# Delta-rule layer on Trainium2: low-rank products, v's transposes and bonus moved to fixed units inside later segments, eight units moved from the score fills to the end of the inverse

## The chip, the cores and the metric

The kernel runs on one core of one Trainium2 chip. The metric is device time of one execution in microseconds (us), the median of 3 runs. One profiled execution, with every instruction recorded, gives the views below.

In the views, PE is the matrix engine (TensorE), PEld its weight loads, DVE the vector engine, ACT the scalar engine, POOL GpSimd, SP the engine that issues transfers. A name such as L753 is line 753 of the kernel before; the changed kernel has line numbers of its own, some 3 to 8 higher.

## The reference, cut to what matters

One layer mixes a causal pooling branch and an RWKV-7 branch (8 heads of 64 channels, 4096 tokens). Only the second bears on the change:

```
seg = h @ w_in[...]                      # r, w_lo, k, v, a_lo, z, each shifted by mu
w_raw = w0 + tanh(w_lo) @ w_up           # low-rank product 1
decay = exp(-exp(-softplus(-w_raw) - 0.5))
a = sigmoid(a0 + a_lo @ a_up)            # low-rank product 2
kk = k*k_k / max(|k*k_k|, L2_EPS)        # per head
S_t = S_{t-1} (diag(decay_t) - kk_t^T (a_t kk_t)) + v_t^T k_t ;  y_t = S_t r_t
y = groupnorm(y)*ln_w + ln_b + sum(r*k*r_k) * v          # the last term is the bonus
out = mix(y * silu(z), pooling branch) @ w_out
```

## The kernel before, in words

A first phase (up to about 394 us of the trace) normalises, projects and pools. Then 16 **blocks** of 256 tokens follow, each of 4 **steps** (chunks of 64 tokens), with 4 head pairs. For block b three pieces run one after the other, written as Python code that the scheduler puts into one fixed queue per engine:

- `scores(b)`: for each of the 4 steps the score products `scp_sc`/`scp_px` (L660), their masking on DVE (L667), copies of the diagonal parts into `stg` on ACT (L675, tile UV). In between stand the finish of the block before (`ytp` transposes L887, the four scaled copies `mx` on ACT L889, two DVE products L890 and L891).
- `inverse(b)`: DVE inverts 32 triangular blocks of 32x32 by a chain of 30 row steps, each a multiply `Wt` (L724) and an add `W` (L729), begun by the transpose `Ab` (L706) and ended by the transposes into `MQ` (L742 to L743). PE then makes `qp` from MQ (L753), ACT copies it, PE makes `m21p` (L761). Ahead of the recurrence come the first products `px` of `lead` (L787).
- `chain(b)`: the recurrence over the 4 steps. A step is: `px` from the state S (L812), copies `xa` on ACT (L819), `psn` (L824), copies into `UV` on ACT (L832), `psn` again (L840), new S on DVE (L846), `px` from UV (L851), copies `y` on ACT (L858). After the steps 1 and 3 the group norm `gn` follows: square `ysq` on ACT (L868), sums `var` on DVE (L870, L871), a power on POOL (L873), the product `y` on DVE (L875).

These three leave PE time. It is filled with `front(b+1)`, the projection of the next block, a generator of **units**; `fill(n)` draws n units. A segment (`seg`, one 128-channel slice kS, rS, vS or zS for each head pair, and one `lo` for the low-rank inputs) is 8 units, and each unit is three fp16 matmuls of 128x257 (L552 to L554) into a tile `pj`; ACT and DVE then take the finished segment out of `pj` (L556, L557). Counts before: 20 units in scores, 88 in the inverse (12 of them by `fill(FT)` behind the row steps, 4 by `fill(FQ)` behind qp), 28 in the chain. The last block has no next front and fills with units of the output projection instead, `run(gp, ceil(n * PF))`.

Besides the segments a head pair needs in its front: the low-rank products `pl` and `pa` (L583, L584), followed by tanh `tw`, `ta`, an addition of one to `tw` (L586 to L589, ACT), a running sum `L` (L591, DVE) and two exponentials `Ppad`, `Pi` (L593, L595, ACT); the products `AR`, `BK` on DVE (L603 to L609); `cent`, which transposes and centres v by two products `vps` (L624) and copies them into UV (L630); `late`, which makes the bonus `pb` (L637) and multiplies it (`bon`, L638). The tiles pj, pl, pa, vps and pb share three buffers `ps_pj`, so a later one waits until ACT or DVE has emptied the earlier ones.

Who goes first when several engines could: PRI raises the inverse's row steps and the chain's copies, and the chain's products are held in the order in which they are written (`ordered`).

Of the kernel before, what the change touches and what calls it, by code (L numbers as in the profile page):

```python
# [10 lines left out]
F32 = mybir.dt.float32  # L11
# [3 lines left out]
AF = mybir.ActivationFunctionType  # L15
ALU = mybir.AluOpType
# [36 lines left out]
def kernel(  # L53
# [23 lines left out]

    FS, FE, FT, FQ, FA, FB, FY = 2, 2, 12, 4, 3, 2, 2
    FI = [4] * 16
# [400 lines left out]
    with ExitStack() as ph:  # L480
# [56 lines left out]
        def front(b, f):  # L537
# [3 lines left out]
            for q in range(2):  # L541
                for hx, tag, src in ((hh, "hh", hT_hi), (hl, "hl", hT_lo)):
                    ht = hp.tile([P, 4, TB2 + 1], F16, tag=tag, name=f"{tag}{b}_{q}")
                    SP.dma_start(ht, src[4 * q : 4 * q + 4, :, a0_:a1_].rearrange("k p t -> p k t"))
                    hx += [ht[:, k, :] for k in range(4)]

            def seg(m, name, bufs=2):
                pp = ps_pj.tile([P, TB2 + 1], F32, tag="pj", name=f"pj{b}_{m}")
                for k in range(KT):
                    if k:  # L550
                        yield
                    unpin(PE.matmul(pp, w2_hi[m][:, k, :], hh[k], start=(k == 0), stop=False))  # L552
                    PE.matmul(pp, w2_hi[m][:, k, :], hl[k], start=False, stop=False)  # L553
                    PE.matmul(pp, w2_lo[m][:, k, :], hh[k], start=False, stop=(k == KT - 1))  # L554
                sg = wk.tile([P, TB2], F32, tag=name, name=f"{name}{b}_{m}", bufs=bufs)
                A.activation(sg, pp[:, 1:], AF.Identity, bias=0.0, scale=c1[:, m : m + 1])  # L556
                V.scalar_tensor_tensor(sg, pp[:, :TB2], c2[:, m : m + 1], sg, op0=ALU.mult, op1=ALU.add)  # L557
                return sg
# [11 lines left out]
            c3 = lambda t_: t_.rearrange("q (c t) -> q c t", c=NCH)  # L570
            todo = []
            sqs = []
            for p in range(NPAIR):
# [6 lines left out]

                ps_ = slice(p * P, (p + 1) * P)
                pl, pa = (ps_pj.tile([P, TB2], F32, tag="pj", name=f"{n}{b}_{p}") for n in ("pl", "pa"))
                PE.matmul(pl, up[0:64, ps_], lo[0:64], start=True, stop=True)  # L583
                PE.matmul(pa, up[64:128, ps_], lo[64:128], start=True, stop=True)  # L584
                tw = wk.tile([P, TB2], F32, tag="tw", name=f"tw{b}_{p}")
                A.activation(tw, pl, AF.Tanh, bias=pv[:, HW0, p : p + 1], scale=0.5)  # L586
                ta = wk.tile([P, TB2], F32, tag="ta", name=f"ta{b}_{p}")
                A.activation(ta, pa, AF.Tanh, bias=pv[:, HA0, p : p + 1], scale=0.5)
                A.activation(tw, tw, AF.Identity, bias=one, scale=1.0)  # L589
                L = wk.tile([P, TB2], F32, tag="L", name=f"L{b}_{p}")  # L590
                V.tensor_tensor_scan(L, rst, tw, 0.0, op0=ALU.mult, op1=ALU.add)  # L591
                Pp = Ppad[p % NPT]
                A.activation(Pp[:, :, 1:], c3(L), AF.Exp, bias=0.0, scale=cexp)  # L593
                Pi = wk.tile([P, TB2], F32, tag="Pi", name=f"Pi{b}_{p}")
                A.activation(Pi, L, AF.Exp, bias=0.0, scale=-cexp)  # L595
                if todo:
                    todo.pop(0)()
                yield
# [11 lines left out]
                G.tensor_copy(pc[:, p, :], Pp[:, :, C])  # L610
                if todo:
                    todo.pop(0)()
                rk = wk.tile([P, TB2], F32, tag="rk", name=f"rk{b}_{p}")
# [7 lines left out]
                def cent(p=p, vS=vS):  # L621
                    vps = ps_pj.tile([P, 4, P], F32, tag="pj", name=f"vps{b}_{p}")
                    for j in range(2):
                        PE.matmul(vps[:, j, :], vS[:, j * P : (j + 1) * P], cmat, start=True, stop=True)  # L624
                    if p == NPAIR - 1:
                        for q in range(NPAIR):
                            PE.matmul(vps[32 * q : 32 * q + 32, 2:4, :], hsel, sqs[q].rearrange("q (j t) -> q j t", j=2), start=True, stop=True)
                        A.copy(ssb.rearrange("q (j t) -> q j t", j=2), vps[:, 2:4, :])
                    for j in range(2):
                        A.copy(  # L630
                            UV[64:128].rearrange("q (c j) e -> q c j e", j=2)[:, :, j, p * P : (p + 1) * P],
                            vps[64 * j : 64 * j + 64, 0:2],
                        )

                def late(p=p, rk=rk, vS=vS):
                    pb = ps_pj.tile([P, TB2], F32, tag="pj", name=f"pb{b}_{p}")
                    PE.matmul(pb, bones, rk, start=True, stop=True)  # L637
                    V.tensor_mul(bon[:, p, :], pb, vS)  # L638

                todo = [cent, late]  # L640
                if p < NPAIR - 1:
                    yield
            f["todo"] = todo
            yield

        def scores(b, f, fill):
# [7 lines left out]
            for ch in range(NCH):  # L654
# [22 lines left out]
                if ch == 2:  # L677
# [8 lines left out]
                    for g in range(2):  # L686
                        V.transpose(d2T[64 * g : 64 * g + 64], d2)
                if ch in (0, 3):
                    f["todo"].pop(0)()
# [82 lines left out]
        def unpin(mm):  # L772
            if pin[0]:
                tc.keep_in_program_order(mm)
                pin[0] = False
# [274 lines left out]
```

## Time and profile before

| | us |
|---|---|
| median of 3 runs (lowest to highest) | 2144.5 (2143.86 to 2147.55) |
| the profiled execution: its time | 2144.86 |
| the profiled execution: its span, first to last instruction | 2143.2 |
| PE busy (share of the span) | 1995.0 (93%) |
| DVE busy | 1410.0 (66%) |
| ACT busy | 1039.2 (48%) |
| POOL busy | 131.9 (6%) |

"Busy" counts the time in which an engine works on at least one instruction; a share is a mean over phases that have different limits. A row of a timeline gives the start, the duration, the engine, the line, the operation with output<-input tiles and shapes, the count, and in brackets the idle time of that engine just before with the instruction that ended it. Windows give the busy time of each engine in a stretch, and PEclk, the clock of the matrix engine that the chip granted there (1.00 is 2.4 GHz, 0.50 is 1.2 GHz).

### The profile page before, as it was taken

What the parts mean: (1) busy time and instruction counts of PE and PEld (TensorE: products, weight loads), DVE (VectorE), ACT (ScalarE), POOL (GpSimd) and SP (SyncE); (2) the same over time, 40 slices, a digit from 0 to 9 for tenths busy, and PEclk for the clock granted to TensorE, in tenths of its full rate; (3) what the DMA queues carried; (4) which work ended last, traced back from release to release, by engine and by line L of the source; (5) the groups of instructions that cost most, each with busy time, mean ns of one, the idle gap of its engine ahead of it and who ended that gap; (6) DMA issues with size and microseconds to landing.
All of it is one profiled execution on the core that took longest, in us unless ns stands there. A gap on an engine that the chain in (4) does not pass through costs nothing.

```text
span 2143.2 us, 48435 instructions
## 1 busy us (share of the span) xinstructions
PE 1995.0 (93%) x20186; PEld 1473.1 (69%) x20186; DVE 1410.0 (66%) x3533; ACT 1039.2 (48%) x2247; POOL 131.9 (6%) x262
## 2 busy tenths in 40 slices
PE   5999999999898998998989989889899889999998
PEld 2444444677777777777777777777777767788886
DVE  7898977465856757758567576685775766533333
ACT  3554433355565565655655556555565563322211
POOL 0000000000000000000000000000000000100000
PEclk8999999999999999999999999999999999999999
DMA  8867667100010110100101101011010334444431
GB/s 311 281 227 232 236 232 256 46 21 25 7 32 2 31 27 6 31 7 26 31 2 31 26 6 32 2 31 27 6 31 26 124 119 139 140 145 138 147 108 69
DMA packets 140445, 183.20 MB, mean 85 GB/s; under 512 B 12097, under 2 KB 94017, under 8 KB 140226
## 3 DMA queue, kind: packets, MB, share of 16 engines
q1 hardware_dynamic: 140226, 180.11, 25.8%
q8 instruction: 158, 2.59, 0.5%
q14 instruction: 61, 0.50, 0.1%
HBM read 121.22 MB, written 58.85 MB: 84 GB/s over the span
## 4 chain that ended last, share of the span: by engine, by line
PE 58%; DVE 27%; ACT 9%; issue 3%; DMA 2%; SPq 1%; POOL 0%; DVEq 0%; ACTq 0%; POOLq 0%
PE po L950 6%; PE pj L552 6%; PE po L952 5%; PE po L951 5%; PE pj L553 5%; PE pj L554 5%; DVE W L729 5%; DVE Wt L724 4%; PE pp L412 4%; PE pp L410 4%; PE pp L411 4%; PE psn L824 2%; PE scp_sc L660 2%; PE px L812 2%; PE vps L624 2%
## 5 line engine op out<-in xcount | busy, mean ns | idle before, releaser
L552 PE MATMUL pj<-hh,w2h 128*128 128x257 f16 x2176 | 612.5, 281 | 18.8 <-DVE rS L557 9.5
L554 PE MATMUL pj<-hh,w2l 128*128 128x257 f16 x2176 | 605.9, 278 | 0.0
L553 PE MATMUL pj<-hl,w2h 128*128 128x257 f16 x2176 | 604.6, 278 | 0.0
L553 PEld LDWEIGHTS <-w2h 128*128 128x128 f16 x2176 | 218.8, 101 | 57.3 <-issue 24.1
L552 PEld LDWEIGHTS <-w2h 128*128 128x128 f16 x2176 | 216.4, 99 | 53.4 <-issue 6.5
L554 PEld LDWEIGHTS <-w2l 128*128 128x128 f16 x2176 | 214.5, 99 | 35.0
L950 PE MATMUL po<-wo,mh 128*128 128x512 f32 x512 | 204.8, 400 | 2.3 <-ACT mh L934 2.3
L951 PE MATMUL po<-wo,mh 128*128 128x512 f32 x512 | 202.0, 395 | 0.0
L411 PE MATMUL pp<-lo,w1h 128*128 128x512 f16 x512 | 194.0, 379 | 1.1 <-DVE lo L225 1.1
L410 PE MATMUL pp<-hi,w1h 128*128 128x512 f16 x512 | 194.1, 380 | 0.2 <-ACT hi L224 0.2
L412 PE MATMUL pp<-hi,w1l 128*128 128x512 f16 x512 | 194.0, 379 | 0.0
L954 DVE TENSOR_TENSOR x<-po,x 128x512 f32<-128x512 f32 x64 | 44.2, 690 | 154.7 <-PE po L952 154.6
L956 ACT ACTIVATE sq<-x 128x512 f32<-128x512 f32 x64 | 40.4, 631 | 211.0 <-DVE x L954 194.3
L729 DVE TENSOR_TENSOR W<-W,Wt 128x30 f32<-128x30 f32 (+7 forms) x480 | 118.2, 246 | 11.2
L724 DVE TENSOR_TENSOR Wt<-W,Ab 128x30 f32<-128x30 f32 (+7 forms) x480 | 117.2, 244 | 10.0
L950 PEld LDWEIGHTS po<-wo,mh 128*128 128x128 f32 x512 | 97.0, 190 | 24.5 <-ACT mh L934 2.6
L951 PEld LDWEIGHTS po<-wo,mh 128*128 128x128 f32 x512 | 96.9, 189 | 22.3
L675 ACT COPY UV<-sc 32x256 f32<-32x256 f32 x128 | 80.8, 631 | 63.5 <-DVE sc L667 62.8
L952 PE MATMUL po<-wo,ml 128*128 128x512 f32 x256 | 101.9, 399 | 0.0
L557 DVE SCALAR_TENSOR_TENSOR kS<-pj,c,kS 128x256 f32<-128x256 f32 x64 | 30.6, 478 | 99.7 <-ACT kS L556 99.7
L412 PEld LDWEIGHTS <-w1l 128*128 128x128 f16 x512 | 50.1, 98 | 61.3 <-issue 1.7
L410 PEld LDWEIGHTS <-w1h 128*128 128x128 f16 x512 | 50.2, 98 | 58.9 <-issue 0.8
(244 smaller groups left out, 3826.0 us busy)
## 6 DMA issues: line engine op xcount, KB each, us to landing
x<-in_x_dram SPq DMA_DIRECT2D x64, 256.0 KB, 3.0
out_dram<-x SPq DMA_DIRECT2D x64, 256.0 KB, 2.1
xk<-in_xT_dram SPq DMA_DIRECT2D x56, 256.0 KB, 3.9
xt<-in_x_dram SPq DMA_DIRECT2D x28, 512.0 KB, 5.9
wada<-in_w_ada_dram SPq DMA_DIRECT2D x24, 512.0 KB, 6.8
w2raw<-in_w_in_dram SPq DMA_DIRECT2D x17, 512.0 KB, 5.8
hh<-hT_hi SPq DMA_DIRECT2D x32, 257.0 KB, 3.8
hl<-hT_lo SPq DMA_DIRECT2D x32, 257.0 KB, 3.0
```

The costliest lines, as they stand in the source:

```text
L410: PE.matmul(pp, w1_hi[m][:, k, :], hi, start=(k == 0), stop=False)
L411: PE.matmul(pp, w1_hi[m][:, k, :], lo, start=False, stop=False)
L412: PE.matmul(pp, w1_lo[m][:, k, :], hi, start=False, stop=(k == KT - 1))
L552: unpin(PE.matmul(pp, w2_hi[m][:, k, :], hh[k], start=(k == 0), stop=False))
L553: PE.matmul(pp, w2_hi[m][:, k, :], hl[k], start=False, stop=False)
L554: PE.matmul(pp, w2_lo[m][:, k, :], hh[k], start=False, stop=(k == KT - 1))
L675: A.copy(stg[o : o + 32, :, i8], sc[o : o + 32, i8, o : o + 32].rearrange("q i t -> q t i"))
L724: V.tensor_mul(tmp[:, :n, :k], W[:, r0:, k : k + 1].to_broadcast([P, n, k]), Ab[:, k : k + 1, :k].to_broadcast([P, n, k]),)
L729: V.tensor_add(W[:, r0:, :k], W[:, r0:, :k], tmp[:, :n, :k])
L950: unpin(PE.matmul(po, mh[:, k, ts_], wo[0][k][n], start=(k == 0), stop=False))
L951: PE.matmul(po, mh[:, k, ts_], wo[1][k][n], start=False, stop=False)
L952: PE.matmul(po, (ml[:, k] if b % 2 == 0 else ml[k])[:, ts_], wo[0][k][n], start=False, stop=(k == KT - 1))
```

## The change

The two low-rank products of a head pair, with all that follows them up to the exponentials, leave the end of the rS segment and stand as a function `lowrank` between units 2 and 3 of the vS segment that follows. `cent` and the bonus of a pair leave the places behind the next rS and vS segment and go to unit 6 of the next kS and of the next rS segment. `vps` shrinks from 4 to 2 slots, since the norms of the keys (products with `hsel`) now have a tile `pn` of their own. What is left over from the last pair (norms, cent, bonus) is drawn by the scores of the block at the steps 0, 1 and 3; before, two pieces (cent with norms, bonus) were drawn at 0 and 3. FS falls from 2 to 1 and FT rises from 12 to 20: eight units go from the scores (20 to 12) to the place behind the row steps (88 to 96 in the inverse). For the last block the same number makes 12 instead of 8 projection units there.

```diff
--- before.py
+++ after.py
@@ -75,7 +75,7 @@
     NCH = TB2 // C
     NI = NCH * NH
 
-    FS, FE, FT, FQ, FA, FB, FY = 2, 2, 12, 4, 3, 2, 2
+    FS, FE, FT, FQ, FA, FB, FY = 1, 2, 20, 4, 3, 2, 2
     FI = [4] * 16
     PF = 0.6
     PRI = 400
@@ -544,11 +544,16 @@
                     SP.dma_start(ht, src[4 * q : 4 * q + 4, :, a0_:a1_].rearrange("k p t -> p k t"))
                     hx += [ht[:, k, :] for k in range(4)]
 
+
+            mid = {3: [], 6: []}
+
             def seg(m, name, bufs=2):
                 pp = ps_pj.tile([P, TB2 + 1], F32, tag="pj", name=f"pj{b}_{m}")
                 for k in range(KT):
                     if k:
                         yield
+                    if mid.get(k):
+                        mid[k].pop(0)()
                     unpin(PE.matmul(pp, w2_hi[m][:, k, :], hh[k], start=(k == 0), stop=False))
                     PE.matmul(pp, w2_hi[m][:, k, :], hl[k], start=False, stop=False)
                     PE.matmul(pp, w2_lo[m][:, k, :], hh[k], start=False, stop=(k == KT - 1))
@@ -568,7 +573,6 @@
             A.activation(lo[0:64], lo[0:64], AF.Tanh)
             yield
             c3 = lambda t_: t_.rearrange("q (c t) -> q c t", c=NCH)
-            todo = []
             sqs = []
             for p in range(NPAIR):
                 kS = yield from seg(1 + 4 * p, "kS")
@@ -578,23 +582,22 @@
                 yield
                 rS = yield from seg(2 + 4 * p, "rS")
 
-                ps_ = slice(p * P, (p + 1) * P)
-                pl, pa = (ps_pj.tile([P, TB2], F32, tag="pj", name=f"{n}{b}_{p}") for n in ("pl", "pa"))
-                PE.matmul(pl, up[0:64, ps_], lo[0:64], start=True, stop=True)
-                PE.matmul(pa, up[64:128, ps_], lo[64:128], start=True, stop=True)
-                tw = wk.tile([P, TB2], F32, tag="tw", name=f"tw{b}_{p}")
-                A.activation(tw, pl, AF.Tanh, bias=pv[:, HW0, p : p + 1], scale=0.5)
-                ta = wk.tile([P, TB2], F32, tag="ta", name=f"ta{b}_{p}")
-                A.activation(ta, pa, AF.Tanh, bias=pv[:, HA0, p : p + 1], scale=0.5)
-                A.activation(tw, tw, AF.Identity, bias=one, scale=1.0)
-                L = wk.tile([P, TB2], F32, tag="L", name=f"L{b}_{p}")
-                V.tensor_tensor_scan(L, rst, tw, 0.0, op0=ALU.mult, op1=ALU.add)
+                tw, ta, L, Pi = (wk.tile([P, TB2], F32, tag=n, name=f"{n}{b}_{p}") for n in ("tw", "ta", "L", "Pi"))
                 Pp = Ppad[p % NPT]
-                A.activation(Pp[:, :, 1:], c3(L), AF.Exp, bias=0.0, scale=cexp)
-                Pi = wk.tile([P, TB2], F32, tag="Pi", name=f"Pi{b}_{p}")
-                A.activation(Pi, L, AF.Exp, bias=0.0, scale=-cexp)
-                if todo:
-                    todo.pop(0)()
+
+                def lowrank(p=p, tw=tw, ta=ta, L=L, Pi=Pi, Pp=Pp):
+                    ps_ = slice(p * P, (p + 1) * P)
+                    pl, pa = (ps_pj.tile([P, TB2], F32, tag="pj", name=f"{n}{b}_{p}") for n in ("pl", "pa"))
+                    PE.matmul(pl, up[0:64, ps_], lo[0:64], start=True, stop=True)
+                    PE.matmul(pa, up[64:128, ps_], lo[64:128], start=True, stop=True)
+                    A.activation(tw, pl, AF.Tanh, bias=pv[:, HW0, p : p + 1], scale=0.5)
+                    A.activation(ta, pa, AF.Tanh, bias=pv[:, HA0, p : p + 1], scale=0.5)
+                    A.activation(tw, tw, AF.Identity, bias=one, scale=1.0)
+                    V.tensor_tensor_scan(L, rst, tw, 0.0, op0=ALU.mult, op1=ALU.add)
+                    A.activation(Pp[:, :, 1:], c3(L), AF.Exp, bias=0.0, scale=cexp)
+                    A.activation(Pi, L, AF.Exp, bias=0.0, scale=-cexp)
+
+                mid[3].append(lowrank)
                 yield
                 vS = yield from seg(3 + 4 * p, "vS")
                 if p == 0:
@@ -608,8 +611,6 @@
                 V.tensor_mul(AR[:, p, :, 1, :], c3(rS), Pp[:, :, 1:])
                 V.tensor_mul(BK[:, p, :, 1, :], c3(ta), c3(Pi))
                 G.tensor_copy(pc[:, p, :], Pp[:, :, C])
-                if todo:
-                    todo.pop(0)()
                 rk = wk.tile([P, TB2], F32, tag="rk", name=f"rk{b}_{p}")
                 V.scalar_tensor_tensor(rk, rS, pv[:, HRK, p : p + 1], ta, op0=ALU.mult, op1=ALU.mult)
                 yield
@@ -619,28 +620,30 @@
                 V.scalar_tensor_tensor(szt[:, p, :], tz, 1.0, zS, op0=ALU.add, op1=ALU.mult)
 
                 def cent(p=p, vS=vS):
-                    vps = ps_pj.tile([P, 4, P], F32, tag="pj", name=f"vps{b}_{p}")
+                    vps = ps_pj.tile([P, 2, P], F32, tag="pj", name=f"vps{b}_{p}")
                     for j in range(2):
                         PE.matmul(vps[:, j, :], vS[:, j * P : (j + 1) * P], cmat, start=True, stop=True)
-                    if p == NPAIR - 1:
-                        for q in range(NPAIR):
-                            PE.matmul(vps[32 * q : 32 * q + 32, 2:4, :], hsel, sqs[q].rearrange("q (j t) -> q j t", j=2), start=True, stop=True)
-                        A.copy(ssb.rearrange("q (j t) -> q j t", j=2), vps[:, 2:4, :])
                     for j in range(2):
                         A.copy(
                             UV[64:128].rearrange("q (c j) e -> q c j e", j=2)[:, :, j, p * P : (p + 1) * P],
-                            vps[64 * j : 64 * j + 64, 0:2],
+                            vps[64 * j : 64 * j + 64],
                         )
 
-                def late(p=p, rk=rk, vS=vS):
+                def bonus(p=p, rk=rk, vS=vS):
                     pb = ps_pj.tile([P, TB2], F32, tag="pj", name=f"pb{b}_{p}")
                     PE.matmul(pb, bones, rk, start=True, stop=True)
                     V.tensor_mul(bon[:, p, :], pb, vS)
 
-                todo = [cent, late]
+                def norms():
+                    pn = ps_pj.tile([P, TB2], F32, tag="pj", name=f"pn{b}")
+                    for q in range(NPAIR):
+                        PE.matmul(pn[32 * q : 32 * q + 32, :], hsel, sqs[q], start=True, stop=True)
+                    A.copy(ssb, pn)
+
+                mid[6] += [cent, bonus]
                 if p < NPAIR - 1:
                     yield
-            f["todo"] = todo
+            f["todo"] = [norms] + mid[6]
             yield
 
         def scores(b, f, fill):
@@ -685,7 +688,7 @@
                     V.reciprocal(d2, d2)
                     for g in range(2):
                         V.transpose(d2T[64 * g : 64 * g + 64], d2)
-                if ch in (0, 3):
+                if ch != 2:
                     f["todo"].pop(0)()
                 fill(FS)
                 if ch % 2 == 0:
```

The order of the instructions is the same in all the blocks 1 to 14, so one block shows it. The names carry the pair or the step as their last small number (`pl_2` is pair 2 of the next block), segments are numbered as they come (`pj_11` is vS of pair 2, `pj_12` zS of pair 2).

On PE, around the first products `qp` of the inverse's end, before:

```order
L553 MATMUL pj_10_9728<-hl_1_9185,w2h_1766 128x257
L554 LDWEIGHTS w2l_1767
L554 MATMUL pj_10_9728<-hh_1_9183,w2l_1767 128x257
L583 MATMUL pl_2_9762<-lo_0_9242,up 128x256
L584 MATMUL pa_2_9763<-lo_0_9242,up 128x256
L753 MATMUL qp_9884<-MQ_9803,sc_9163 32x32 x9
L624 MATMUL vps_1_9776<-cmat,vS_7_9620 128x128 x2
L552 LDWEIGHTS w2h_1770
```

In the changed kernel the same low-rank products stand inside segment 11, not behind segment 10:

```order
L558 MATMUL pj_11_9799<-hl_0_9185,w2h_1770 128x257
L559 LDWEIGHTS w2l_1771
L559 MATMUL pj_11_9799<-hh_0_9183,w2l_1771 128x257
L591 MATMUL pl_2_9809<-lo_0_9261,up 128x256
L592 MATMUL pa_2_9810<-lo_0_9261,up 128x256
L557 LDWEIGHTS w2h_1770
L557 MATMUL pj_11_9799<-hh_0_9183,w2h_1770 128x257
```

And the products `qp` stand behind those of `lead`, all 32 together, after segment 12:

```order
L790 MATMUL px_0_9879<-UV_7977,sc_9167 64x64
L790 MATMUL px_1_9880<-UV_7977,sc_9167 64x64
L756 MATMUL qp_9889<-MQ_9766,sc_9167 32x32 x32
L557 LDWEIGHTS w2h_2167
L557 MATMUL pj_13_9926<-hh_0_9183,w2h_2167 128x257
```

So `qp` moved from ahead of segment 11 to behind segment 12 and `lead`, and the products of v (`vps_1`) no longer follow it.

On ACT, in the chain from the low-rank pieces of pair 3 to the copies `UV` of step 2, before:

```order
L588 ACTIVATE ta_3_10125<-pa_3_10120,pv 128x256
L589 ACTIVATE tw_3_10123<-tw_3_10123,one 128x256
L630 COPY UV_9191<-vps_2_10133 64x2x128 x2
L593 ACTIVATE Ppad_3665<-L_3_10128 128x4x64
L595 ACTIVATE Pi_3_10131<-L_3_10128 128x256
L858 COPY y_0_9972<-px_0_9874 64x4x64
L858 COPY y_0_9972<-px_1_9875 64x4x64
L868 ACTIVATE ysq_0_10160<-y_0_9972 128x512
L604 ACTIVATE ta_3_10125<-ta_3_10125,pv 128x256
L819 COPY xa_2_10192<-px_0_9874 64x256
L819 COPY xa_2_10192<-px_1_9875 64x256
L832 COPY UV_7974<-psn_2_10174 64x4x64 x2
```

In the changed kernel the two `y` copies and the square come ahead of them, and the exponentials `Ppad` and `Pi` of pair 3 stand directly ahead of the copies of `psn_2`:

```order
L861 COPY y_0_9977<-px_0_9879 64x4x64
L861 COPY y_0_9977<-px_1_9880 64x4x64
L871 ACTIVATE ysq_0_10158<-y_0_9977 128x512
L822 COPY xa_2_10190<-px_0_9879 64x256
L822 COPY xa_2_10190<-px_1_9880 64x256
L593 ACTIVATE tw_3_10132<-pl_3_10196,pv 128x256
L594 ACTIVATE ta_3_10133<-pa_3_10197,pv 128x256
L595 ACTIVATE tw_3_10132<-tw_3_10132,one 128x256
L597 ACTIVATE Ppad_3665<-L_3_10134 128x4x64
L598 ACTIVATE Pi_3_10135<-L_3_10134 128x256
L835 COPY UV_7977<-psn_2_10172 64x4x64 x2
```

On DVE, in the same stretch, before (the running sum `L_3` first, the group norm's product `y_0` eight rows later):

```order
L591 SCALAR_TENSOR_TENSOR L_3_10128<-rst,tw_3_10123 128x256
L846 SCALAR_TENSOR_TENSOR S<-psn_1_10061,pc_7973,Sd_1_10108 128x64 x4
L603 SCALAR_TENSOR_TENSOR tb_3_10272<-ta_3_10125,kS_13_10024 128x256
L836 TENSOR_TENSOR Sd_2_10223<-S,pc_7973 128x256
L605 SCALAR_TENSOR_TENSOR AR_9187<-kS_13_10024,vec,Ppad_3665 128x4x64
L870 TENSOR_REDUCE var_0_10162<-ysq_0_10160 128x8
L606 SCALAR_TENSOR_TENSOR BK_9430<-tb_3_10272,pv,Pi_3_10131 128x4x64
L871 TENSOR_SCALAR var_0_10162<-var_0_10162 128x8
L607 TENSOR_TENSOR ta_3_10125<-ta_3_10125,kS_13_10024 128x256
L875 TENSOR_TENSOR y_0_9972<-y_0_9972,rstd_0_10165 128x512
```

In the changed kernel the running sum stands behind that product:

```order
L839 TENSOR_TENSOR Sd_2_10231<-S,pc_7976 128x256
L873 TENSOR_REDUCE var_0_10160<-ysq_0_10158 128x8
L874 TENSOR_SCALAR var_0_10160<-var_0_10160 128x8
L878 TENSOR_TENSOR y_0_9977<-y_0_9977,rstd_0_10163 128x512
L596 SCALAR_TENSOR_TENSOR L_3_10134<-rst,tw_3_10132 128x256
L608 SCALAR_TENSOR_TENSOR AR_9191<-kS_13_10034,vec,Ppad_3665 128x4x64
L606 SCALAR_TENSOR_TENSOR tb_3_10280<-ta_3_10133,kS_13_10034 128x256
L611 TENSOR_TENSOR AR_9191<-rS_14_10129,Ppad_3665 128x4x64
L609 SCALAR_TENSOR_TENSOR BK_9444<-tb_3_10280,pv,Pi_3_10135 128x4x64
```

So `UV` of step 2 moved behind `Ppad_3` and `Pi_3`, which read `L_3`, and `L_3` moved behind `y_0`.

## Rows read from the trace of the kernel before

**Rows 1.** The page, busy time by engine: us, share of span, instructions.
```profile
PE 1995.0 (93%) x20186; PEld 1473.1 (69%) x20186; DVE 1410.0 (66%) x3533; ACT 1039.2 (48%) x2247; POOL 131.9 (6%) x262
```

**Rows 2.** Waits of PE, 420 to 1720 us: us in total, times, longest.
```profile
PE qp L753 <- DVE MQ L743: 40.9, 15, 2.9
PE vps L624 <- ACT tw L586: 17.3, 32, 0.6
PE btp L716 <- ACT BT L717: 11.9, 15, 1.0
PE pj L552 <- DVE rS L557: 9.5, 15, 0.9
...
```

**Rows 3.** Timeline of PE, the first qp of four inverses.
```profile
667.24 0.52 PE L753 MATMUL qp<-MQ,sc 32*32 32x32 f32 x18 [2.89 <-DVE MQ L743]
754.65 0.37 PE L753 MATMUL qp<-MQ,sc 32*32 32x32 f32 x18 [2.89 <-DVE MQ L743]
840.76 0.44 PE L753 MATMUL qp<-MQ,sc 32*32 32x32 f32 x17 [2.89 <-DVE MQ L743]
1705.08 0.52 PE L753 MATMUL qp<-MQ,sc 32*32 32x32 f32 x18 [2.90 <-DVE MQ L743]
```

**Rows 4.** Windows: inverse up to MQ, then two stretches behind a qp.
```profile
718.54:754.60 36.06, 30.70 (x252) 24.94 (x250) 33.91 (x102) 17.87 (x38) 1.60 (x7) 1.00 0.03 8
755.51:758.92 3.41, 3.41 (x18) 2.41 (x18) 2.59 (x6) 2.24 (x6) 0.43 (x1) 0.50 0.02 5
667.30:675.00 7.70, 7.70 (x56) 5.88 (x57) 4.04 (x10) 3.51 (x9) 0.79 (x2) 0.59 0.02 3
```

**Rows 5.** Timeline of PE, units at full clock and the products of v.
```profile
736.38 0.27 PE L553 MATMUL pj<-hl,w2h 128*128 128x257 f16 x1
736.49 0.27 PE L554 MATMUL pj<-hh,w2l 128*128 128x257 f16 x1
...
737.95 0.71 PE L624 MATMUL vps<-cmat,vS 128*128 128x128 f32 x4 [0.56 <-ACT tw L586]
```

**Rows 6.** Timeline of DVE: ahead of the inverse, then step 2 of the chain.
```profile
718.54 0.69 DVE L890 TENSOR_TENSOR mx<-mx,bon 128x512 f32<-128x512 f32 x1 [1.62 <-ACT mx L889]
...
722.38 1.24 DVE L706 STREAM_TRANSPOSE Ab<-UV 64x1024 f32<-64x1024 f32 x1 [0.62 <-ACT UV L675]
...
778.33 0.69 DVE L591 TENSOR_TENSOR_SCAN L<-rst,tw 128x256 f32<-128x256 f32 x1 [0.90 <-ACT tw L589]
...
784.31 0.69 DVE L875 TENSOR_TENSOR y<-y,rstd 128x512 f32<-128x512 f32 x1 [1.53 <-POOL rstd L873]
```

**Rows 7.** Timeline of ACT: the mx copies, then chain step 2.
```profile
717.01 1.50 ACT L889 ACTIVATE mx<-ytp,pv 128x128 f32<-128x128 f32 x4
...
764.61 1.53 ACT L755 COPY MQ<-qp 32x256 f32<-32x256 f32 x4
...
779.43 0.40 ACT L595 ACTIVATE Pi<-L 128x256 f32<-128x256 f32 x1
779.85 0.76 ACT L858 COPY y<-px 64x256 f32<-64x256 f32 x2
...
783.60 0.75 ACT L832 COPY UV<-psn 64x256 f32<-64x256 f32 x2 [0.96 <-PE psn L824]
```

**Rows 8.** Timeline of POOL, the group norm's power in step 2.
```profile
782.54 1.74 POOL L873 TENSOR_TENSOR rstd<-var,nhalf 128x8 f32<-128x8 f32 x1 [2.77 <-DVE var L871]
```

**Rows 9.** Timeline of PE: lead, the first products of three steps, psn of step 2.
```profile
763.04 0.68 PE L787 MATMUL px<-UV,sc 64*64 64x64 f32 x16
...
766.83 0.69 PE L812 MATMUL px<-S,AR 64*64 64x64 f32 x32
...
772.82 1.08 PE L812 MATMUL px<-S,AR 64*64 64x64 f32 x32
...
780.27 0.33 PE L812 MATMUL px<-S,AR 64*64 64x64 f32 x2
...
784.40 0.69 PE L840 MATMUL psn<-UV,BT 128*64 128x64 f32 x16
```

## The prediction

> **What bounds the kernel now.** The page says that PE is busy for 93% of the span and DVE for 66% [rows 1]. Read alone, that says that only PE's idle time and slow time can be won. PE's waits in the 16 blocks come next [rows 2]: the four largest sum to 79.6 us, and 40.9 of that is one wait, `qp` for DVE's MQ, 15 times. Its last end is always DVE. So the third view is the window that ends at MQ: DVE is busy for 33.91 of 36.06 us there while PE is at 1.00 of its clock with 30.70 busy [rows 4]. In that stretch DVE, not PE, sets the end: whatever PE saves before MQ only lengthens its wait for MQ. From MQ on, PE, ACT and DVE take turns along the recurrence: lead 763.04, step 0 766.83, step 1 772.82, step 2 780.27, `psn` of step 2 784.40 [rows 9].
>
> The fourth thing to see is the clock. Behind the wait of 2.89 at 754.65, PE runs at 0.50 (1.2 GHz) for 3.41 us [rows 3, 4]: 16 units wait behind it, and the slow stretch costs about 3.41 x 0.5 = 1.7 us; I use 1.6. Behind the qp at 667.24 it is longer: 7.70 us at a mean of 0.59 lose 3.2 us [rows 4], and the period to the next qp is 87.41 against 86.11 for the next one [rows 3]. So one fall of the clock costs 1.6 to 2.9 (1.6 + 1.3). The ten periods from 840.76 to 1705.08 have a mean of 86.43 [rows 3], 0.3 over the block that I reckon with (754.65 to 840.76).
>
> **The change part by part**, for one such block, along the chain that sets its end.
>
> *Scores, −0.9.* Six of the eight units that leave stand ahead of the last score product. Three matmuls each, 0.11 us apart [rows 5], make 0.33 a unit, 2.0 in all. But what follows waits for ACT: DVE's `mx` waited 1.62 for the four copies of 1.50, and `Ab` then 0.62 for the `stg` copy [rows 6, 7]. ACT's copies and tanh stand in one queue ahead of mx, so I take a bit under half. Bounds 0 and −2.0.
>
> *Inverse up to MQ, +1.05.* The row steps are the same work. Three things join DVE's path or delay it: the evacuation of a kS segment that came before Ab until now (0.4, estimated between nothing and the 0.69 of a product or sum of DVE [rows 6]), ACT's copy of Ab behind BT copies (0.3), and the later running sum and its products that now fall between row steps (0.5 net of gaps that close, less 0.2). DVE has only 36.06 − 33.91 = 2.15 idle to take them [rows 4]. Bounds 0 and +1.9. The waits of PE that vanish here (`vps` for tw, 0.56 at 737.95 [rows 5]) lie under DVE's path and are worth nothing; new ones, of pa and pj for an emptied buffer, lie there too.
>
> *MQ to lead, −2.5.* Before: 754.65 to 763.04, 8.39 [rows 3, 9], in which stand 16 units (5.3), vps, pb, part of qp and 1.6 of slow clock. After, units stand ahead of lead and qp behind it, so PE has work when it would have waited, and the wait of 2.89 goes. How many units are left when MQ is there: 16, and the 8 that join, less the 12 that fit into 2.89 and the 1.05 that the path is longer (3.94 / 0.33), and 1 back for new waits: 13. They take 4.3, a low-rank pair 0.65, and a segment that DVE and ACT must take out of its buffer about 0.95 (two pieces of 0.4 to 0.5): 5.9 at full clock. Bounds: 4.3 and 8.39 − 1.6 = 6.8.
>
> *Lead to step 0, +0.7.* All 32 qp now stand behind lead, and ACT's copies of qp (1.53 at 764.61 [rows 7]) wait behind tanh of z, which waits for a segment on DVE. 3.79 becomes 4.5. Bounds 0 and +1.5. Step 0 itself keeps its 6.0 (766.83 to 772.82), within 0.1.
>
> *Step 1, −1.6.* It took 7.45 (772.82 to 780.27 [rows 9]), against 6.0 for step 0, since pl, pa, their tanh and vps stood in it. These leave for step 2, a pb enters: 5.85.
>
> *Step 2, +2.1: a new wait.* The order puts ACT's `UV` copies of psn_2 behind Ppad_3 and Pi_3, these wait for the running sum L_3, and that stands on DVE behind the group norm's product `y_0`. The link of y_0 can be read before: `y` copied at 779.85, the power 782.54 to 784.28 on POOL, the product at 784.31, for which DVE waited 1.53 [rows 6 to 8]. So 4.46 from copy to product, 4.05 without the BK product that stood between. Then 0.6 for y_0, 0.7 for L (0.69 [rows 6]), 0.4 each for Ppad and Pi (0.40 [rows 7]), 0.75 for UV [rows 7] and `psn` starts. The y copies came 779.85 − 772.82 = 7.03 after step 1's first px [rows 7, 9]; less the 1.6 that step 1 loses, and the 0.3 by which Ppad and Pi held them, 5.1. 5.1 + 4.05 + 0.6 + 0.7 + 0.8 + 0.8 = 12.05, against 784.40 − 772.82 = 11.58 before [rows 9]. So of the 1.6 won in step 1, 2.1 is given back in step 2. Queued behind UV on ACT are `ta` and the y copies; PE has no units that may pass its psn, so it idles for about 2.2. Bounds: 0 (the sum comes before psn_2 is ready) to 2.6.
>
> An in-order queue is what this term rests on. [...] The row of y_0 agrees: the AR product behind it starts only after it.
>
> *Sum.* −0.9 + 1.05 − 2.5 + 0.7 − 1.6 + 2.1 = −1.15, with 0.1 of step 0 −1.05. The 0.3 by which the mean block is longer than mine, from the long slow stretches, goes too: −1.4. Against this stands the clock: a new idle of 2.2 in step 2, below the 2.89 that made it fall at each qp [rows 3]. The rows show falls behind 2.89, and none in the window at 1.00, which holds the wait of 0.56 [rows 4, 5]; 2.2 is nearer to the former, but products of other tiles still run around it. I take half the blocks at about 1.2: +0.6. So −0.8 a block, 15 blocks, −12, and −0.7 in the first front, where the waits for tanh have no cover. From the profiled 2144.86 (0.3 above the median, 1.7 above its span): 2132.
>
> **The rivals.**
>
> *PE is the bound (0.05).* Then every wait that goes is won: 79.6 [rows 2] and 15 slow stretches at 1.6 to 2.9, 44 at most, so about 2144.9 − 79.6 − 44 = 2021. For it speaks the 93%; against it DVE's 33.91 of 36.06 [rows 4].
>
> *The wait of step 2 isn't paid (0.12).* If L_3 comes in time, 2.1 and the 0.6 of the clock fall away: −3.5 a block, 2144.9 − 52 = 2092. Against it is y_0's wait for POOL [rows 6].
>
> *What is won is given back at the start (0.17).* If Ab starts no earlier than before, since stg's last copies stand behind mx on ACT, −0.9 becomes 0: +0.1 a block, 2146. From a gain there of under 0.1 it is no change. For it speaks that mx and stg, not PE, released DVE [rows 6]; against it that PE's products come 2.0 earlier.
>
> *Slower: the clock falls in each block anew (0.21).* If the idle of 2.2 ahead of psn_2 drops the clock as the 2.89 did, each block pays 1.6 to 2.9: −1.4 + 1.6 = +0.2 to −1.4 + 2.9 = +1.5, so 2148 to 2167. It decides from a price of 1.7 on. For it: after each qp wait the clock fell [rows 3, 4]. Against it: the wait is shorter.
>
> [...]
>
> **How the numbers follow.** The forecast has 0.45: 2132, own range 2118 to 2142, from the bounds of step 0's lead and the clock (half to none of the price either way). A measurement of this kernel tells about 0.2% (4.3 us) from no change, so faster is below 2140.2 and slower above 2148.8. Faster: 0.41 of the forecast, the first two rivals' 0.17 and 0.02 of the third, 0.60. Same: 0.04, 0.11 of the third and 0.03 of the fourth, 0.18. Slower: 0.04 and 0.18, 0.22. For 8 in 10 I leave out the first rival, half of the second and the upper quarter of the fourth: 2092 to 2156.
>
> **What would show it.** The wait of qp for MQ is gone and MQ to lead is near 6; the period of the blocks is 85 to 86; DVE from mx to MQ takes 1 longer; a wait of psn for UV, near 2, 15 times, heads PE's list; the running sum of pair 3 follows y_0. The prediction is wrong if step 1 and 2 together shrink, if MQ isn't there when PE gets to qp, or if the windows at 0.50 stand behind another wait in every block.

## The result, and the profile after

The changed kernel takes 2114.24 us (2112.71 to 2114.56), the kernel before 2145.56 on the same occasion: a ratio of 0.9852 with a 95% interval of 0.9835 to 0.9869. That is 31 us faster, where 12.5 were forecast: the right side, but 2.5 times the gain. It lies below the forecast's own range (2118 to 2142) and inside the wider one for 8 in 10 (2092 to 2156).

The page of the changed kernel, busy time by engine:

```profile
PE 1979.8 (94%) x20186; PEld 1460.1 (69%) x20186; DVE 1404.4 (66%) x3533; ACT 1045.7 (50%) x2247; POOL 130.8 (6%) x262
```

Its waits of PE, 420 to 1690 us, beside [rows 2]:

```profile
PE psn L843 <- ACT UV L835: 23.3, 14, 1.7
PE btp L719 <- ACT BT L720: 17.4, 15, 1.2
PE pj L557 <- DVE kS L562: 13.5, 14, 1.0
PE pa L592 <- DVE rS L562: 13.0, 29, 0.5
PE pl L591 <- DVE bon L635: 8.8, 29, 0.3
PE qp L756 <- DVE MQ L746: 1.9, 1, 1.9
```

The 40.9 us of `qp` for MQ are gone but for one wait of 1.9, and `psn` for UV in step 2, which did not exist, heads the list. It is 1.7 us long, where an idle of about 2.2 was forecast. The rows of the block that begins with `Ab` at 799.79, PE first (the end of the inverse, then steps 1 and 2):

```profile
831.33 0.27 PE L557 MATMUL pj<-hh,w2h 128*128 128x257 f16 x1 [0.96 <-DVE kS L562]
832.78 0.70 PE L591 MATMUL pl<-lo,up 64*128 64x256 f32 x2 [0.30 <-DVE bon L635]
838.35 0.68 PE L790 MATMUL px<-UV,sc 64*64 64x64 f32 x16
848.26 0.32 PE L815 MATMUL px<-S,AR 64*64 64x64 f32 x2
854.14 0.42 PE L815 MATMUL px<-S,AR 64*64 64x64 f32 x5
860.30 0.51 PE L843 MATMUL psn<-UV,BT 128*64 128x64 f32 x10 [1.66 <-ACT UV L835]
```

ACT, DVE and POOL in the same block:

```profile
853.47 0.75 ACT L861 COPY y<-px 64x256 f32<-64x256 f32 x2 [0.61 <-PE px L854]
859.22 0.40 ACT L598 ACTIVATE Pi<-L 128x256 f32<-128x256 f32 x1
859.52 0.73 ACT L835 COPY UV<-psn 64x256 f32<-64x256 f32 x2
```
```profile
831.19 1.22 DVE L746 STREAM_TRANSPOSE MQ<-UV 32x1024 f32<-32x1024 f32 x1
832.35 0.37 DVE L635 TENSOR_TENSOR bon<-pb,vS 128x256 f32<-128x256 f32 x1
857.57 0.69 DVE L878 TENSOR_TENSOR y<-y,rstd 128x512 f32<-128x512 f32 x1 [1.75 <-POOL rstd L876]
858.18 0.68 DVE L596 TENSOR_TENSOR_SCAN L<-rst,tw 128x256 f32<-128x256 f32 x1
```
```profile
855.90 1.64 POOL L876 TENSOR_TENSOR rstd<-var,nhalf 128x8 f32<-128x8 f32 x1 [19.20 <-DVE var L874]
```

Read it backwards: `psn` at 860.30 waits for UV, UV stands behind Pi at 859.22, that reads L of 858.18, which follows `y` at 857.57, for which DVE sat idle 1.75 until POOL was done. From step 1's first px (848.26) to this psn are 12.04 us; the prediction worked out 12.05.

The windows that matter for the clock and the inverse follow; each row has the stretch, its length, the busy time and count of PE, PEld, DVE, ACT and POOL, then PEclk. PEclk is a share; the rates behind it are measured in the kernel before. At 1.00 the 128x512 matmuls of the first phase start 0.216 us apart (330.12 to 333.79), 2.4 columns a ns, and at 0.50 the 128x257 ones behind `qp` 0.215 apart (755.56 to 758.57), 1.2 columns a ns: the 2.4 and 1.2 GHz given with it are these two rates. Changed kernel, 5.1 us up to the end of MQ; from Ab to MQ; a stretch behind the new wait.

```profile
827.30:832.40 5.10, 4.14 (x35) 3.24 (x33) 5.06 (x9) 2.83 (x7) 0.51 (x1) 1.00 0.00 0
799.79:831.19 31.40, 28.36 (x232) 23.33 (x233) 29.81 (x97) 16.03 (x35) 1.10 (x6) 1.00 0.01 4
861.65:865.07 3.42, 3.42 (x45) 2.38 (x44) 2.84 (x9) 2.90 (x9) 0.00 (x0) 0.50 0.02 5
```

The same first two stretches of the kernel before:

```profile
749.50:754.60 5.10, 2.26 (x14) 1.23 (x11) 4.91 (x8) 2.05 (x4) 0.47 (x1) 1.00 0.00 0
722.38:753.37 30.99, 26.86 (x223) 21.99 (x222) 29.47 (x95) 14.92 (x33) 1.14 (x6) 1.00 0.01 3
```

PE now works for 4.14 of the last 5.1 us of the inverse (2.26 before), and no stretch at 0.50 stands behind MQ any more. In 10 of the blocks 0 to 14 one stands behind the wait of step 2 (and one in step 0 of block 14). The starts of `Ab`, MQ, lead, the steps' first px and the first score product give the stages, for a block of before (Ab at 722.38, one fall of the clock, the short one) and one of the changed kernel without a fall (Ab at 884.42):

| stage, us | before | after | measured | forecast |
|---|---|---|---|---|
| first score product to Ab | 18.31 | 17.26 | −1.05 | −0.9 |
| Ab to MQ | 30.99 | 31.40 | +0.41 | +1.05 |
| MQ to lead (of before with the slow units) | 9.67 | 7.17 | −2.50 | −2.5 |
| lead to step 0 | 3.79 | 3.91 | +0.12 | +0.7 |
| step 0 | 6.00 | 5.99 | 0 | +0.1 |
| step 1 | 7.45 | 5.88 | −1.57 | −1.6 |
| step 2 | 6.47 | 8.38 | +1.91 | +2.1 |
| step 3 to the next score product | 3.44 | 3.56 | +0.12 | 0 |
| sum | 86.12 | 83.55 | −2.57 | −1.05 |
| mean period less this block (clock) | +0.33 | +0.75 | +0.42 | +0.3 |

The means of the 13 periods from block 1 to block 14 are 86.45 and 84.30: 2.15 a block, 28 us in all. Ahead of the first `Ab` 2.6 us are won (459.76 instead of 462.35; 0.7 was forecast), block 0 loses 0.7 of them, and about 1 comes behind block 14.

### The profile page after: what moved, and what is told of

The parts are those of the page before. It is cut to its first block, busy times and chain, and to the rows that moved or that the text cites. A ratio compares the mean times of both kernels' runs of the same rounds, so it can differ in the third digit from the quotient of the medians.

```text
span 2112.3 us, 48406 instructions
## 1 busy us (share of the span) xinstructions
PE 1979.8 (94%) x20186; PEld 1460.1 (69%) x20186; DVE 1404.4 (66%) x3533; ACT 1045.7 (50%) x2247; POOL 130.8 (6%) x262
## 4 chain that ended last, share of the span: by engine, by line
PE 47%; DVE 31%; ACT 13%; issue 4%; DMA 2%; POOL 1%; SPq 0%; ACTq 0%; DVEq 0%; POOLq 0%
PE po L953 6%; PE po L955 6%; PE po L954 6%; DVE Wt L727 5%; DVE W L732 4%; PE pp L412 4%; PE pp L411 4%; PE pp L410 4%; PE pj L557 3%; PE pj L558 2%; PE pj L559 2%; DVE sc L670 2%; PE scp_sc L663 2%; DVE L L596 2%; ACT UV L678 2%
## 5 line engine op out<-in xcount | busy, mean ns | idle before, releaser
L557 PE MATMUL pj<-hh,w2h 128*128 128x257 f16 x2176 | 604.3, 278 | 14.3 <-DVE kS L562 13.5
L559 PE MATMUL pj<-hh,w2l 128*128 128x257 f16 x2176 | 598.1, 275 | 0.0
L558 PE MATMUL pj<-hl,w2h 128*128 128x257 f16 x2176 | 596.6, 274 | 0.0
L557 PEld LDWEIGHTS <-w2h 128*128 128x128 f16 x2176 | 213.1, 98 | 69.1 <-issue 27.4
L558 PEld LDWEIGHTS <-w2h 128*128 128x128 f16 x2176 | 215.6, 99 | 47.8 <-issue 17.0
```

## The experiments

Three theories were at stake. **Theory A**: lead, the chain and the score stage each end with what stands last in a queue, as the prediction has it, and the eight moved units alone give most of the gain. **Theory B**: the new places, those of the low-rank products above all, are what keeps PE at work near MQ. **Theory C**: PE's total work is the bound and waits show only slack. Edits are against the kernel named.

### The two parts of the change apart

Kernel before, fills alone:

```diff
-    FS, FE, FT, FQ, FA, FB, FY = 2, 2, 12, 4, 3, 2, 2
+    FS, FE, FT, FQ, FA, FB, FY = 1, 2, 20, 4, 3, 2, 2
```

> The kernel before with FS = 1 and FT = 20 alone; low-rank products, v's transposes and bonus stay where they were, and the first qp stay ahead of segment 11. Theory 1 (chain of ends: scores up to Ab, DVE up to MQ, then the units left on PE): 1.05 a block less before Ab as in the changed kernel, 0.4 more in the inverse; PE has 6 more units (2.0 us) ahead of qp, so the wait for MQ falls from 2.89 to about 0.9, the clock does not fall behind it (1.6 and, on average, 0.3 saved), and the step-2 wait of the changed kernel does not exist: about 2.5 a block, 2107 (2098 to 2115), faster than the changed kernel. Theory 2 (the moved low-rank products are what takes the wait and the clock's fall away): the falls stay and only the scores gain, about 0.7 a block, 2135 (2128 to 2140).

Measured: 2139.54, ratio 0.9965 (0.9952 to 0.9978). The scores give their 1.05, the inverse costs 0.5, and the wait of qp for MQ is down to 0.4, all as theory 1 had it. The time is that of theory 2 all the same: the clock falls in each of the blocks 1 to 14, at 0.50 for 3.4 or 6.8 us behind MQ. MQ to lead does not shrink (9.99 in the block shown). PE's idle has not gone, it stands in pieces ahead of `pa` and `qp`:

```profile
751.62 0.70 PE L584 MATMUL pa<-lo,up 64*128 64x256 f32 x2 [1.19 <-DVE kS L557]
752.76 0.26 PE L753 MATMUL qp<-MQ,sc 32*32 32x32 f32 x8 [0.44 <-DVE MQ L743]
```
```profile
747.60:752.70 5.10, 3.53 (x24) 2.28 (x22) 4.92 (x8) 1.64 (x4) 0.51 (x1) 1.00 0.00 0
```

Changed kernel with FS = 2, FT = 12, the new places alone:

> The changed kernel with FS = 2 and FT = 12 as before: the new places alone. Theory 1: against the changed kernel 1.05 a block is lost before Ab; on PE 6 units (2.0 us) fewer stand between Ab and lead, so MQ to lead falls from 5.9 to about 3.9: 0.95 a block less, 2100 (2092 to 2108), with the step-2 wait of UV as it is. Theory 2 (the eight units behind the row steps are what pays, because PE runs dry at MQ without them): the clock falls behind a new wait for MQ or the scores cost more than they give, 2130 (2118 to 2142).

Measured: 2141.87, 0.9986 (0.9976 to 0.9995). Theory 1 fails here too. Six units fewer stand ahead of lead, but without a fall (block 1) MQ to lead shrinks by 0.33 only (6.83 against 7.16), since PE stops at `pl` until DVE has done `bon`, which stands behind the row steps:

```profile
PE pl L591 <- DVE bon L635: 30.5, 28, 1.3
```

PE works 3.40 of the last 5.1 us there, and the clock falls behind MQ in each of the blocks 2 to 14:

```profile
750.68:755.78 5.10, 3.40 (x24) 2.23 (x21) 4.92 (x8) 2.04 (x4) 0.46 (x1) 1.00 0.02 3
```

So each part alone is worth 3 to 6 us, both together 31.

### Which of the moved pieces

Changed kernel, `lowrank()` called at the end of rS instead of `mid[3].append(lowrank)`:

> The changed kernel, but the low-rank products of each pair back at the end of its rS segment; v's transposes, bonus and the fills (FS = 1, FT = 20) as changed. Theory (PE runs dry at the low-rank products of pair 2, which wait for buffers that DVE empties late behind the row steps, and the clock falls behind it): waits and fall near MQ come back as in the kernel with the fills alone, 1.6 to 2 a block, while step 2 keeps no wait for UV: 2130 (2122 to 2140). Rival (v's transposes and bonus carry the gain): 2080 to 2100, as the step-2 wait is not there either.

Measured: 2103.83, 0.98 (0.9784 to 0.9817): neither number, and faster than the changed kernel. The fall near MQ is there in 8 of the blocks 1 to 14 only (here a block without and one with it); step 1 keeps the low-rank products (6.52 instead of 5.88), and step 2, without the wait, takes 6.81.

```profile
740.38:745.48 5.10, 3.60 (x27) 2.53 (x24) 4.92 (x9) 2.36 (x5) 0.53 (x1) 1.00 0.01 3
823.30:828.40 5.10, 3.60 (x27) 2.53 (x24) 4.91 (x9) 2.35 (x5) 0.52 (x1) 1.00 0.00 0
```

Against the fills alone the mean period is 2.20 shorter (83.81 for 86.01): 1.42 between MQ and lead, 0.78 in the steps.

Changed kernel, `cent` and bonus called at the end of the next rS and vS:

> The changed kernel, but v's transposes and bonus at their places of before; the low-rank products and the fills (FS = 1, FT = 20) as changed. Theory (the low-rank products' place is what keeps PE from running dry near MQ): no fall of the clock near MQ, the step-2 wait stays, step 1 longer by the transposes (0.5): 2118 (2112 to 2126). Rival (both moves are needed for it): the clock falls near MQ, 2130 to 2145.

Measured: 2159.86, 1.0069 (1.0045 to 1.0094), slower than before. Both falls appear in most blocks, mostly 6.8 us behind MQ and 3.4 in step 2, since `pj` waits up to 2.0 for kS near MQ and the new wait of step 2 stays:

```profile
PE pj L557 <- DVE kS L562: 25.8, 13, 2.0
PE psn L848 <- ACT UV L840: 23.7, 15, 1.7
```

So, with the fills, the move of v's transposes and bonus gives the gain (these two were not tried apart, nor without the fills). That of the low-rank products to unit 3 does two things: the falls near MQ that are left in 8 of 14 blocks go (none in the changed kernel), and the wait in step 2 comes, which costs more. The run with pair 3 at unit 5 (2082.78, next section) has the first without the second, and is 21 us faster than the run without the move (2103.83). Theory A fails, and theory B is right of the places as a whole, not of the low-rank products above all.

### The wait of step 2

Changed kernel, pair 3's low-rank products at unit 5:

```diff
-                mid[3].append(lowrank)
+                mid[3 if p < NPAIR - 1 else 5].append(lowrank)
```

> The changed kernel with the low-rank products of pair 3 alone at unit 5 instead of 3 of its vS segment, so that on ACT the UV copies of step 2 come ahead of tanh, Ppad and Pi of pair 3. Theory 1 (UV of step 2 waits in the queue behind Ppad and Pi, these for L_3, and L_3 for the group norm's product): the wait of psn for UV goes, step 2 falls from 8.4 to about 6.5, and the clock does not fall there: 1.9 + 0.7 = 2.6 a block, 2076 (2068 to 2084). Theory 2 (PE's work bounds step 2 and the wait only shows slack): 2110 to 2116.

Measured: 2082.78, 0.9706 (0.9691 to 0.972). UV now comes ahead of tanh on ACT, psn at once behind it:

```profile
849.39 0.74 ACT L835 COPY UV<-psn 64x256 f32<-64x256 f32 x2 [0.96 <-PE psn L827]
850.16 0.47 ACT L593 ACTIVATE tw<-pl,pv 128x256 f32<-128x256 f32 x1
```
```profile
792.46:874.74 82.28, 77.71 (x1060) 62.07 (x1060) 58.72 (x168) 49.98 (x116) 5.94 (x11) 1.00 0.08 21
```

Step 2 takes 6.52 (8.38), 0.6 comes back in step 3, where the products now stand, and the clock is at 1.00 through all of the blocks 1 to 13. The mean period is 82.29: 2.0 less than in the changed kernel, where 2.6 were expected; the step-3 share was overlooked. Theory C, which expected 2110 to 2116, is out.

The same pair at unit 1:

> The changed kernel with the low-rank products of pair 3 alone at unit 1 instead of 3 of its vS segment: its products and tanh come earlier, but L_3 still follows the group norm's product on DVE, and Ppad and Pi still stand ahead of the UV copies of step 2. Theory 1 (the group norm's product is the link): unchanged within 5, 2109 to 2119, the wait of psn for UV stays near 1.7. Theory 2 (the low-rank products of pair 3 themselves come too late): the wait goes, 2076 to 2090.

Measured: 2142.95, 0.9986 (0.9977 to 0.9996), 29 us slower than the changed kernel. Tanh is early, and the wait grows to 3.0, so lateness of the products is not the cause. But "unchanged" was wrong: ACT's queue also has `ta`, which reads a product of DVE behind L, ahead of UV here, and step 1 takes the products back (6.62):

```profile
866.98 0.60 ACT L607 ACTIVATE ta<-ta,pv 128x256 f32<-128x256 f32 x1 [0.59 <-DVE tb L606]
867.60 0.75 ACT L835 COPY UV<-psn 64x256 f32<-64x256 f32 x2
```

With 3.0 of idle the clock falls in step 2 of each of the blocks 0 to 14. This is the mechanism of the prediction's slower rival, in another kernel, though the time stays below the 2148 that it gave.

Changed kernel with useless products in that wait (`for _ in range(16)`: 128x128 fp16 into psn):

> The changed kernel with 16 fp16 matmuls of 128x128 without use put on PE ahead of psn of step 2, whose place is written over by psn itself: PE works for some 1.3 of the 1.7 in which it waits for UV. Theory 1 (idle makes the clock fall, and the falls in two of three blocks cost 1.1 each): no falls in step 2, the wait for UV itself stays paid, 83.54 a block: 2103 (2100 to 2107). Theory 2 (falls come from elsewhere): 2112 to 2118.

Measured: 2126.73, 0.9917 (0.9902 to 0.9932), neither theory. It tells nothing of the clock: the products write the tile that the UV copies read, so they waited for UV themselves and stand behind the wait, as 1 us more of work:

```profile
862.94 1.46 PE L843 MATMUL psn<-w2h 128*128 128x128 f16 x16 [1.66 <-ACT UV L835]
```

### The clock near MQ

Kernel before, `pa` of pair 2 made three and nine times over, a control and a filled wait (the edit for nine; the control has 3 in its place):

```diff
-                PE.matmul(pa, up[64:128, ps_], lo[64:128], start=True, stop=True)
+                for _ in range(9 if p == 2 else 1):
+                    PE.matmul(pa, up[64:128, ps_], lo[64:128], start=True, stop=True)
```

> The kernel before with the low-rank product pa of pair 2 made three times over (two repeats, 0.6 us of PE work that changes nothing). It also puts all qp behind lead, so that behind pa the products vps of v are next. Control for the next run. Theory 1 (PE's idle near MQ makes the clock fall; the wait moves from qp to vps, which needs a buffer that tanh empties at MQ's end) and theory 2 (the fall has nothing to do with that idle) both: a wait of about 2.3 at vps, falls as before, 2145 (2138 to 2150). Theory 3 (the wait of qp for MQ as such costs): 2105 to 2115.

> As the run before, with pa of pair 2 made nine times over, 2.5 us of PE work in the place of the wait near MQ. Theory 1 (PE's idle near MQ makes the clock fall): the wait falls to about 0.5, the clock stays up, 1.6 for the slow units and 0.3 for the longer slow stretches are saved: 1.95 a block, 2116 (2110 to 2124), though PE does more. Theory 2: the falls stay, 2145 (2140 to 2152).

Measured on one chip: 2145.9 (1.0002, 0.9993 to 1.0012) and 2125.98 (0.9913, 0.9898 to 0.9928). In the control the wait only moves, from `qp` to the products of v, and the falls stay:

```profile
756.52 0.85 PE L625 MATMUL vps<-cmat,vS 128*128 128x128 f32 x4 [2.37 <-ACT tw L587]
```
```profile
751.03:756.13 5.10, 3.12 (x17) 1.96 (x15) 4.91 (x8) 2.05 (x4) 0.47 (x1) 1.00 0.00 0
```

With the wait filled PE works all of the last 5.1 us, the clock does not fall in the blocks 1 to 13, and their period is 84.61 instead of 86.46:

```profile
755.56:760.66 5.10, 5.10 (x28) 4.03 (x26) 4.92 (x8) 2.05 (x4) 0.47 (x2) 1.00 0.00 0
```

More work on PE is 20 us faster than less. The 1.85 a block are nearly the 1.95 expected; the total gains less, since the profile loses 8.5 us ahead of the second block (Ab of block 1 at 559.21, 550.69 in the control), where the clock is at 0.50 for 10.24 us behind MQ of block 0.

### What sets lead

Pair 3 at unit 5 (2082.78) with FS = 2 and FT = 12:

> The kernel with pair 3 at unit 5 (2082.8) with FS = 2 and FT = 12. Theory 1 (without the six units more, PE catches up with DVE near MQ and waits for pl and pa, and the clock falls behind that, as with the new places alone): falls near MQ in every block; 86.5 a block of that kernel less the 2.0 of the step-2 wait: 84.5, 2113 (2105 to 2122). Theory 2 (the falls there follow from the step-2 wait of UV): no falls, 1.0 lost before Ab and 2.0 won behind MQ, 2069 (2063 to 2076).

Measured: 2105.05, 0.9806 (0.9791 to 0.982), at the edge of theory 1. Falls near MQ, without any wait of UV, but from block 4 on in every second block only; period 82.86 without and 84.4 with. So the falls near MQ do not follow from step 2, and the units behind the row steps are worth 22 us here.

Pair 3 at unit 5, with ACT's and DVE's emptying of each segment and `bon` inside `tc.high_priority(offset=2 * PRI)`:

> The kernel with pair 3 at unit 5 (2082.8), with the pieces that empty the three buffers (ACT's and DVE's copy of each segment, bonus product) put ahead of the row steps by priority, so that on DVE the segment kS of pair 2 is emptied ahead of the last transposes into UV. Theory 1 (in the changed kernel lead follows from PE's units and its waits for buffers, MQ comes 5.9 earlier than it is needed): PE's wait of 1.2 at segment 11 goes, MQ a little later costs nothing, 1.0 to 1.5 a block, 2064 (2058 to 2072). Theory 2 (DVE up to MQ sets the end): MQ later by 0.3 to 0.5, 2088 (2083 to 2094).

Measured: 2116.76, 0.9866 (0.985 to 0.9881), slower than either theory. The wait of 1.0 for kS goes, but PE only gets sooner to `pl`, and waits there for `bon`, which is still behind MQ:

```profile
PE pl L592 <- DVE bon L637: 33.7, 29, 2.2
```

MQ comes 0.4 later and lead 0.4 later (7.17 from MQ to lead without a fall, as ever), the scores lose 0.7, and with 2.2 in one piece the clock falls in 11 of the blocks 1 to 14.

All pairs at unit 5 (`mid = {5: [], 6: []}`):

> The changed kernel with the low-rank products of all four pairs at unit 5 instead of 3 of their vS segment. Theory 1 (lead follows from the end of MQ and of the bonus product behind it on DVE, for which pl of pair 2 waits, then from the units that are left on PE): two units fewer are left behind pl, so MQ to lead is 0.6 to 0.7 shorter than with pair 3 alone at unit 5 (2082.8): 2073 (2068 to 2078). Theory 2 (PE's work bounds the stretch, the place of pl doesn't matter): 2080 to 2086.

Measured: 2080.01, 0.9695 (0.9679 to 0.9711), the lowest time, but its interval overlaps with that of pair 3 alone, and it lies where theory 2 put it. The rows decide for theory 1: MQ to lead is 6.50 for 7.16, its 0.66. But 0.56 comes back between lead and step 0: lead at 832.12 comes earlier ahead of segment z's tanh, and ACT's copies of qp stand behind that tanh, which waits for DVE. The period falls by 0.31, with 0.22 from a shorter inverse (31.18).

```profile
833.94 0.42 ACT L619 ACTIVATE tz<-zS 128x256 f32<-128x256 f32 x1 [1.24 <-DVE zS L562]
834.38 1.53 ACT L758 COPY MQ<-qp 32x256 f32<-32x256 f32 x4
```

## Why the prediction was right in direction and wrong in size

**The chain terms** scores, steps 0 to 2 and MQ to lead came out within 0.2 each. The new wait of UV, its place, its chain over POOL and `y`, and the length of step 2 were read from the order and rows of before alone. That a copy does not pass in its engine's queue, on which the wait rests, shows in the block above: the `psn` products that UV copies had ended by 857.42, ACT sat idle for 1.59 until L let Ppad start at 858.89, and UV's copies began only behind Pi, at 859.52.

**The step that failed is "Inverse up to MQ, +1.05".** It measured +0.41. The windows show why: DVE's instructions from Ab to MQ go from 95 to 97, its busy time from 29.47 to 29.81, its idle time from 1.52 to 1.59. The kS evacuation that joins (0.44) is the whole cost. ACT's late copy of Ab (0.3) held the first row step by 0.22, but that step starts 3.84 behind Ab, 4.19 before (726.57), since the running sum no longer stands ahead of it. And this sum (0.5) is no addition: it stood ahead of the first row step before (725.04) and stands between two now (807.08). The first row is of before, the others are of the changed kernel:

```profile
725.04 0.68 DVE L591 TENSOR_TENSOR_SCAN L<-rst,tw 128x256 f32<-128x256 f32 x1
803.63 0.19 DVE L727 TENSOR_TENSOR Wt<-W,Ab 128x30 f32<-128x30 f32 x1 [0.22 <-ACT Ab L711]
807.08 0.68 DVE L596 TENSOR_TENSOR_SCAN L<-rst,tw 128x256 f32<-128x256 f32 x1
```

**"Lead to step 0, +0.7"** was the second: +0.12. The mechanism exists, but the kernel before paid for it already: there too the copies of qp (764.61) stood behind tanh of z. That tanh starts 1.13 behind lead before (763.04) and 1.26 after (838.35), and this difference is the +0.12 (the rows are of before, then after):

```profile
764.17 0.42 ACT L618 ACTIVATE tz<-zS 128x256 f32<-128x256 f32 x1 [0.55 <-DVE zS L557]
839.61 0.42 ACT L619 ACTIVATE tz<-zS 128x256 f32<-128x256 f32 x1 [0.68 <-DVE zS L562]
```

Where lead moves ahead of that tanh, as with all pairs at unit 5 (1.82), it costs: +0.56 over the changed kernel. These two terms are 1.2 of the 1.5 by which the sum was short; with them right the forecast would have been about 2114. The first front, sized at −0.7, gave −2.6, less 0.7 lost in block 0.

**MQ to lead, −2.5, was right for a wrong reason.** I counted 13 units as what is left of a budget (16 + 8 − 12 + 1). In fact 13 units stand behind `pl` of pair 2 in the queue, and `pl` waits for `bon`, the instruction behind MQ on DVE; that the two counts agree is luck. So the stretch is bon, the low-rank pair and 13 units, nearly whatever is moved ahead: six units fewer changed it by 0.33, MQ 0.4 later moved lead by 0.4, and two units fewer behind pl shortened it by 0.66.

**The clock** term took half of the blocks at 1.2 (+0.6); it was 10 of 15 blocks at 1.1, behind 1.7 of idle. That PE's idle near MQ causes the fall is shown by the filled wait. That the wait of 2.89 as one piece matters is not: 1.57 us idle in pieces of up to 1.2 still made it fall in each block with the fills alone.

**The rivals.** "PE is the bound" (2021) is refuted by the filled wait, where more work on PE takes less time. "The wait of step 2 isn't paid" (2092) is what pair 3 at unit 5 makes true, at 2083. "Given back at the start" did not happen: −1.05 in all eight profiles with FS = 1 in which the emptying was left where it was. "The clock falls in each block" held at 3.0 of idle in step 2, not at 1.7.

**Open:** why equal idle makes the clock fall in some blocks and not in others (3.39 and 3.40 us of work in the last 5.1 in two blocks of the run with FS = 2 and pair 3 at unit 5, at 829.77 with and at 914.15 without a fall):

```profile
824.67:829.77 5.10, 3.39 (x24) 2.23 (x21) 4.92 (x8) 2.04 (x4) 0.46 (x1) 1.00 0.00 0
909.05:914.15 5.10, 3.40 (x24) 2.24 (x21) 4.92 (x8) 2.04 (x4) 0.46 (x1) 1.00 0.01 2
```

When a wait comes seems to matter beside its length: in the kernel before, with PE at work for 2.26 or 2.27 of the last 5.1 us in each of the blocks 1 to 14, the slow stretch is 6.83 long in every third of them (2, 5, 8, 11, 14) and 3.41 in the others. No run moved a wait in time alone to show it.

That idle causes the falls in step 2 was argued from the run without that wait, which has none, and the run with 3.0; the run that should have filled it did not.

## What to carry to other kernels

Cost a moved instruction by the set of instructions in the window that sets the end: count what joins and what leaves; a change of order inside it was worth nothing here. Ask of each wait that you charge for whether the kernel before has it too. Look for the first instruction behind the bottleneck's end that a queue on another engine waits for; what stands behind that is the length of the next stretch, whatever is moved ahead. And price PE's idle with its clock: here 2.5 us of useless products in a wait were worth 1.85 a block, and two changes that alone gave 3 and 6 us gave 31 together, because only both kept PE at work near MQ in every block.

## What the runs showed of the hardware that was not expected

Idle that is spread counts: with PE at work for 3.53 of the last 5.10 us before MQ, idle in pieces of up to 1.2, the granted clock fell to 0.50 in every block (fills alone), with 3.60 in 8 of 14 (transposes and bonus with the fills), with 4.14 in none (the changed kernel). The order is not strict: 3.40 gave a fall in each of 13 blocks in one kernel (new places alone) and in every second one in another. And a matmul into a PSUM tile waited for a copy that reads other columns of that tile (862.94, idle 1.66 behind UV) in this program's dependencies, so a filler needs a tile of its own.
